# A hybrid decoder layer on one core: the last mean square on ScalarE, two weight tiles split earlier, and a pair of attention heads one tile later

## The chip, the core and the metric

The kernel runs on one core of a Trainium2 chip. The metric is the device time of one execution, in microseconds, as the median of several runs. The core's engines each work through their own list of instructions in order: TensorE (PE; PEld is its loading of the stationary operand), VectorE (DVE), ScalarE (ACT), GpSimd (POOL), and SyncE (SP), which here only starts DMAs. They wait for each other through semaphores.

## The reference

One decoder layer over 256 tokens of width 2048 in float32:

```
u   = RMSNorm_pre_mix(h);  P = u @ W_in      # z | x,B,C | dt | q | k | v
SSD half: conv + SiLU, chunked state space scan, gate, grouped RMSNorm
attention half, 16 heads of 128: softmax(q k / sqrt(128) + mask) v
h   = h + RMSNorm_post_mix(concat(SSD, attn) @ W_out)
h   = h + RMSNorm_post_mlp(relu(RMSNorm_pre_mlp(h) @ W_up)**2 @ W_down)

def rmsnorm(x, w):
    return x * rsqrt(mean(x * x, axis=-1) + 1e-6) * w
```

The three dilations of the attention are done as one softmax per head, with the logarithm of a key's count as its mask.

## The kernel before

**Products.** Every large product is made of three products of 32-bit operands that were rounded to a high part and a low part: high by high, high by low, low by high (`row_tile`, lines 323 to 325; `seven`, lines 406 to 408, uses a scheme with seven products for eight; `products`, lines 468 and 471, is the form with features on the partitions). So each weight tile of 256 rows by 512 columns goes through the same steps: `fetch` starts its DMA on SP's queue into one of four buffers `raw` (line 158), then `split` makes `hi` on ScalarE (line 144) and `lo` on VectorE (line 145). `parts` gives `hi` and `lo` out of five pairs of buffers, so ScalarE can run up to five tiles ahead of TensorE and then waits until TensorE has used the oldest.

**What sets the order.** Most of the program is put in order by a scheduler that follows priorities; weights have the highest. Two stretches are written out by hand, in an order that every engine keeps (`manual_schedule`): the start, and `mix_to_up`, the passage from the product with `w_out` to that with `w_up`.

**The heads.** `attention` is a generator that treats two heads at a time, in three stages: scores (lines 849, 850) and softmax (lines 857 to 863); the transposes of the softmax (line 871) and their copies; the product with v (lines 880, 881). `heads` puts two such pairs, called A and B below, into the list `waiting`. While a projection runs through its eight weight tiles, `gemm_features` calls `pump` after each tile, as often as the tuple `pumps` says (used in turn); each call takes one stage, of A and B in alternation. All of a pair's scores need both of the two small PSUM buffers (`psmall`), and so do its transposes.

**`mix_to_up`.** There are two tiles of 128 tokens, t = 0 and 1, and four blocks of 512 columns, n = 0 to 3. `out(t, i)` multiplies the last four tiles of `w_out`; `mix` adds that to what was there (line 1080); `mix_square` takes the sum of squares on ScalarE (line 1084); `weight` multiplies by the norm's weights (line 1087); `scale_of` turns the sums into the scale `rm` by a small VectorE operation (`mean`, line 1023) and a power on GpSimd (`rmix`, line 1024); `add` adds the scaled block to h (line 1091); `turn` transposes h on TensorE (line 1100); `take` splits it into the operand of the next product (lines 146, 147); `weigh(i)` fetches and splits tile i of `w_up`; `rows(t, i)` multiplies with it (lines 323 to 325 again). TensorE must have blocks of h to turn before it can begin with `rows`.

**`finish`.** After the very last product, `finish(t, acc)` adds the last block of columns (line 1309), takes its mean square together with the first three blocks' sum on VectorE (line 1311), takes the root on ScalarE and the reciprocal on VectorE (`inverse_root`, lines 1011 and 1012), multiplies the block by its weights in place (line 1313), scales everything, adds h (line 1326) and starts the output's DMAs. For t = 1 the first block of columns goes by ScalarE and TensorE (lines 1317 to 1323).

Of the kernel before, what the change touches and what calls it, by code (L numbers as in the profile page):

```python
# [13 lines left out]
AF = mybir.ActivationFunctionType  # L14
ALU = mybir.AluOpType
# [62 lines left out]
def hymba_layer(ctx: ExitStack, tc: tile.TileContext, x, norm_mix_pre, w_in, conv_w, conv_b, dt_bias, a_log,  # L78
# [909 lines left out]
    qk.append(keys_by_tokens(1, (0, 2, 1, 4, 3, 7, 5), (6,), *eight))  # L988
    vs = two_values(0, *eight[::-1])
    heads(0, *qk[0], vs[0])  # L990
    q2 = queries(COL_Q + 2 * NB, rbq, (1, 1, 0))
    drain()
    heads(1, *qk[1], vs[1])
    qk.append((q2, queries(COL_K + 2 * NB, rbc, (1, 1, 0))))
# [14 lines left out]
    def inverse_root(dst, m):  # L1009

        nc.scalar.activation(m, m, AF.Sqrt)
        nc.vector.reciprocal(dst, m)
# [42 lines left out]
    def mix_to_up(c0, ks, acc):  # L1055


        up = [bank() for _ in range(NT)]
        banks, turned = [], {}
        weighed = hp.tile([P, NT, NB], F32, name="e")  # L1060
        room_w = big.tile([P, SUMS, 2, S], F32R, name="ua").rearrange("p k b s -> p k (b s)")

        def tile_of(src, k, c0, at=None):
            raw = fetch(src, k * KB, c0)
            hi, lo = parts() if at is None else (room_w[:, at + KB * i:at + KB * (i + 1)] for i in range(2))
            split(hi, lo, raw)
            return hi, lo

        def out(t, i):
            row_tile(acc[1 + 2 * t], t, o[i], ks[i], part, False, i == len(ks) - 1)  # L1070

        def weigh(i):
            w[i] = tile_of(w_up, i % 8, i // 8 * NB)

        def rows(t, i):
            row_tile(up[t], t, w[i], i, act_u, i == 0, i == NK // KB - 1)

        def mix(t, n):
            m = mw_at(t, columns(n))
            nc.vector.tensor_tensor(m, acc[n - 2 + 2 * t], m, op=ALU.subtract if n % 2 else ALU.add)  # L1080

        def mix_square(t, n):
            junk = hp.tile([P, NB], F32, name="junk")
            nc.scalar.activation(junk, mw_at(t, columns(n)), AF.Square, accum_out=ssq[:, t, n:n + 1])

        def weight(t, n):
            nc.vector.tensor_mul(mw_at(t, columns(n)) if n == 2 else weighed[:, t], mw_at(t, columns(n)), wpost[n])

        def add(t, n):
            cs = columns(n)  # L1090
            nc.vector.scalar_tensor_tensor(of_h(t, cs), weighed[:, t] if n == 3 else mw_at(t, cs), rm[:, t:t + 1],
                                           of_h(t, cs), op0=ALU.mult, op1=ALU.add)

        def turn(t, n):
            if len(banks) < 3:
                banks.append([bank() if banks else psmall() for _ in range(2)])
            p = turned[t, n] = banks[len(turned) % 3]
            for f in range(4):
                k = 4 * n + f
                nc.tensor.transpose(p[f % 2][:, f // 2 * P:(f // 2 + 1) * P], of_h(t, slice(k * P, (k + 1) * P)), ident)  # L1100

        def take(t, i):
            for k in (2 * i, 2 * i + 1):
                f = k % 4
                split(*(u(k)[:, b, t * P:(t + 1) * P] for b in range(2)),
                      turned[t, k // 4][f % 2][:, f // 2 * P:(f // 2 + 1) * P], w_mlp[:, k:k + 1])

        def square(t, n):
            junk = hp.tile([P, NB], F32, name="junk")
            nc.scalar.activation(junk, of_h(t, columns(n)), AF.Square, accum_out=ssh[:, t, n:n + 1])  # L1110

        o, w = {}, {}
        with tc.high_priority(offset=AHEAD), tc.manual_schedule():
            o[0] = tile_of(w_out, ks[0], c0)
            with tc.issue_after(product[0].ins), tc.issue_after(product[1].ins):
                out(0, 0)
            o[1] = tile_of(w_out, ks[1], c0)
            out(0, 1)
            o[2] = tile_of(w_out, ks[2], c0, 0)
            o[3] = tile_of(w_out, ks[3], c0, 4)  # L1120
            mix(0, 2)
            mix_square(0, 2)
            out(0, 2)
            mix(1, 2)
            mix_square(1, 2)
            first3[0] = sums_but_last(ssq, 0)
            first3[1] = sums_but_last(ssq, 1)
            out(0, 3)
            mix(0, 3)
            weight(0, 2)  # L1130
            weigh(0)
            out(1, 0)
            mix_square(0, 3)
            out(1, 1)
            scale_of(rm, ssq, first3[0], 0)
            weigh(1)
            add(0, 0)
            out(1, 2)
            add(0, 1)
            turn(0, 0)  # L1140
            weigh(2)
            square(0, 0)
            out(1, 3)
            new_u()
            take(0, 0)
            square(0, 1)
            mix(1, 3)
            turn(0, 1)
            take(0, 1)
            take(0, 2)  # L1150
            rows(0, 0)
            mix_square(1, 3)
            rows(0, 1)
            scale_of(rm, ssq, first3[1], 1)
            add(0, 2)
            take(0, 3)
            add(1, 0)
            weigh(3)
            square(0, 2)
            weight(1, 3)  # L1160
            rows(0, 2)
            add(1, 1)
            square(1, 0)
            turn(1, 0)
            turn(0, 2)
            take(1, 0)
            rows(0, 3)
            take(0, 4)
            take(1, 1)
            turn(1, 1)  # L1170
            rows(1, 0)
            square(1, 1)
            rows(1, 1)
            weight(1, 2)
            take(1, 2)
            add(1, 2)
            weigh(4)
            turn(1, 2)
            add(1, 3)
            take(0, 5)  # L1180
            take(1, 3)
            rows(1, 2)
            rows(0, 4)
            turn(1, 3)
            square(1, 2)
            weight(0, 3)
            add(0, 3)
            take(1, 4)
            rows(1, 3)
            weigh(5)  # L1190
            take(1, 5)
            weigh(6)
            turn(0, 3)
            rows(1, 4)
            rows(0, 5)
            take(1, 6)
            square(0, 3)
            weigh(7)
            take(0, 6)
            rows(1, 5)  # L1200
            take(0, 7)
            square(1, 3)
            rows(1, 6)
            scale_of(rmlp, ssh, sums_but_last(ssh, 0), 0)
            rows(0, 6)
            weigh(8)
            take(1, 7)
            rows(0, 7)
            rows(1, 7)
            scale_of(rmlp, ssh, sums_but_last(ssh, 1), 1)  # L1210
        for t in range(NT):
            waiting.append(first_hidden(t, up[t]))
        pump(NT)
        return w[8]
# [87 lines left out]
    def finish(t, acc):  # L1302


        with tc.high_priority(offset=(1 + t) * AHEAD):
            cs = columns(3)
            m, some = (cp.tile([P, 1], F32, name="mean", bufs=2) for _ in range(2))
            nc.vector.tensor_scalar(some, first3[t], 1.0 / D, None, op0=ALU.mult)
            nc.vector.tensor_add(mw_at(t, cs), acc, mw_at(t, cs))
            junk = hp.tile([P, NB], F32, name="junk")  # L1310
            nc.vector.tensor_tensor_reduce(junk, mw_at(t, cs), mw_at(t, cs), 1.0 / D, some, ALU.mult, ALU.add, m)
            inverse_root(rff[:, t:t + 1], m)
            nc.vector.tensor_mul(mw_at(t, cs), mw_at(t, cs), wpost[3])
            if t:
                p = psmall()
                with tc.issue_after(product[t].ins):
                    nc.tensor.matmul(p, ident, of_h(t, columns(0)), start=True, stop=False)
                dg = cp.tile([P, P], F32, name="dg", bufs=2)
                nc.scalar.activation(dg, ident, AF.Copy, scale=rff[:, t:t + 1])
                nc.tensor.matmul(p, dg, mw_at(t, columns(0)), start=False, stop=True)  # L1320
                o = tmp()
                nc.scalar.activation(o, p, AF.Copy)
                nc.scalar.dma_start(ot[:, t, columns(0)], o)
            pieces = (slice(512, 768), slice(768, 1024), slice(1024, 1536), slice(1536, 2048))
            for n, cs in enumerate(pieces if t else (columns(0), *pieces)):
                nc.vector.scalar_tensor_tensor(of_h(t, cs), mw_at(t, cs), rff[:, t:t + 1], of_h(t, cs),
                                               op0=ALU.mult, op1=ALU.add)
                (nc.sync if t else (nc.sync, nc.scalar)[n % 2]).dma_start(ot[:, t, cs], of_h(t, cs))
# [133 lines left out]
```

## Time and profile before

| what | value |
|---|---|
| median of 3 runs | 1464.41 us (1463.12 to 1464.65) |
| the profiled execution: its own time | 1462.01 us |
| its span, first to last instruction | 1460.1 us |
| granted TensorE clock, mean | 0.999 |
| TensorE busy | 1451.3 us, 99% of the span |
| VectorE busy | 1254.7 us, 86% |
| ScalarE busy | 888.7 us, 61% |
| GpSimd busy | 143.1 us, 10% |

The stretches that the change touches lie, on the profile's axis from the span's start, at 446 to 474 us (the first two pairs of heads), at 757 to 800 us (`mix_to_up`) and from 1446 us to the end (`finish`). A row of the timeline reads: start, duration, engine, line, operation, written tile <- read tiles, shapes, and in brackets how long the engine had been idle and what ended that. A matmul's duration is its whole way through the array, 0.39 us for 512 columns, while one starts every 0.23 us; so TensorE loses more in a gap than the bracket shows.

### The profile page before, as it was taken

How to read it: one execution, taken by the hardware profiler on the slowest of the kernel's cores; microseconds unless marked ns; L12 is line 12 of the kernel's file. 1: busy time of each engine (PE TensorE's matmuls, PEld its weight loads, DVE VectorE, ACT ScalarE, POOL GpSimd, SP SyncE). 2: the span in 40 equal slices, each digit the busy share in tenths (PEclk: the TensorE clock that was granted, in tenths of full speed). 3: DMA queues.
4: the chain of work that ended last, by engine and by line, in shares of the span. 5: the costliest groups of instructions: out<-in, count | busy, mean ns of one | idle time of the engine just before them, and what ended most of it. 6: DMA issues, size and time to landing. Idle time of an engine off the chain costs nothing.

```text
span 1460.1 us, 20264 instructions
## 1 busy us (share of the span) xinstructions
PE 1451.3 (99%) x7129; PEld 1223.8 (84%) x7129; DVE 1254.7 (86%) x1864; ACT 888.7 (61%) x1214; POOL 143.1 (10%) x208
## 2 busy tenths in 40 slices
PE   9999999999999999999999999999999999999998
PEld 8888888888888888888887888888888888888886
DVE  6798797898887686689979999988889999999987
ACT  7475675465566555555557677655455776766553
POOL 0003100212010000000100011000111111001000
PEclk9999999999999999999999999999999999999999
DMA  8766666666886586688867798778888888797763
GB/s 273 209 204 180 180 184 192 175 180 184 226 241 206 134 245 199 192 265 253 253 190 241 202 315 240 217 214 230 246 236 271 263 244 250 204 308 238 251 212 116
DMA packets 168039, 323.53 MB, mean 222 GB/s; under 512 B 15185, under 2 KB 18113, under 8 KB 167937
## 3 DMA queue, kind: packets, MB, share of 16 engines
q1 hardware_dynamic: 144448, 272.37, 59.0%
q0 software_dynamic: 15616, 36.19, 12.3%
q10 hardware_dynamic: 7872, 13.68, 2.8%
q8 instruction: 56, 0.92, 0.2%
q14 instruction: 47, 0.38, 0.1%
HBM read 317.96 MB, written 40.41 MB: 245 GB/s over the span
## 4 chain that ended last, share of the span: by engine, by line
PE 99%; DVE 1%; ACT 0%; issue 0%; POOL 0%
PE acc L468 15%; PE acc L323 12%; PE acc L325 12%; PE acc L324 12%; PE acc L471 8%; PE acc L408 6%; PE acc L407 6%; PE acc L406 6%; PE ps L325 3%; PE ps L323 3%; PE ps L324 3%; PE ps L406 2%; PE ps L408 2%; PE ps L407 2%; PE ps L802 1%; PE acc L1375 1%
## 5 line engine op out<-in xcount | busy, mean ns | idle before, releaser
L144 ACT ACTIVATE hi<-raw 128x1024 fp32r<-128x1024 f32 (+1 forms) x408 | 427.1, 1051 | 293.0 <-PE acc L325 93.9
L145 DVE TENSOR_TENSOR lo<-raw,hi 128x1024 fp32r<-128x1024 f32 (+1 forms) x408 | 496.2, 1220 | 103.8 <-ACT hi L144 99.2
L468 PE MATMUL acc<-ua,hi 128*128 128x512 f32 x600 | 163.4, 401 | 0.0
L468 PEld LDWEIGHTS acc<-ua,hi 128*128 128x128 f32 x600 | 105.7, 189 | 16.7
L144 ACT ACTIVATE hi<-e 128x1024 fp32r<-128x1024 f32 x61 | 64.9, 1063 | 73.8 <-DVE e L247 67.4
L323 PE MATMUL acc<-hi,ua 128*128 128x512 f32 x248 | 98.5, 397 | 0.0
L471 PEld LDWEIGHTS acc<-ua,lo 128*128 128x128 f32 x600 | 88.2, 189 | 10.2
L325 PE MATMUL acc<-hi,ua 128*128 128x512 f32 x248 | 96.8, 390 | 0.0
L324 PE MATMUL acc<-lo,ua 128*128 128x512 f32 x248 | 96.7, 390 | 0.0
L471 PE MATMUL acc<-ua,lo 128*128 128x256 f32 x600 | 90.8, 281 | 0.0
L323 PE MATMUL acc<-hi,sh 128*128 128x512 f32 x224 | 88.4, 395 | 0.0
L325 PE MATMUL acc<-hi,sl 128*128 128x512 f32 x224 | 87.3, 390 | 0.0
L324 PE MATMUL acc<-lo,sh 128*128 128x512 f32 x224 | 87.2, 389 | 0.0
L145 DVE TENSOR_TENSOR lo<-e,hi 128x1024 fp32r<-128x1024 f32 x61 | 74.2, 1217 | 0.0
L468 PE MATMUL acc<-uc,hi 128*128 128x512 f32 x240 | 68.4, 397 | 0.0
L406 PE MATMUL acc<-hi,ah 128*128 128x512 f32 x166 | 64.7, 389 | 0.0
L407 PE MATMUL acc<-lo,ah 128*128 128x512 f32 x166 | 64.6, 389 | 0.0
L408 PE MATMUL acc<-hi,al 128*128 128x512 f32 x166 | 64.6, 389 | 0.0
L325 PE MATMUL acc<-hi,al 128*128 128x512 f32 x148 | 57.6, 389 | 0.0
L323 PE MATMUL acc<-hi,ah 128*128 128x512 f32 x148 | 57.6, 389 | 0.0
L324 PE MATMUL acc<-lo,ah 128*128 128x512 f32 x148 | 57.6, 389 | 0.0
L325 PEld LDWEIGHTS acc<-hi,ua 128*128 128x128 f32 x248 | 46.6, 188 | 10.0
(533 smaller groups left out, 3436.4 us busy)
## 6 DMA issues: line engine op xcount, KB each, us to landing
raw<-in_w_in_dram SPq DMA_DIRECT2D x181, 512.0 KB, 4.0
raw<-in_w_down_dram SPq DMA_DIRECT2D x73, 512.0 KB, 5.0
raw<-in_w_up_dram SPq DMA_DIRECT2D x65, 512.0 KB, 4.8
raw<-in_w_out_dram SPq DMA_DIRECT2D x39, 512.0 KB, 4.9
pair<-in_w_up_dram POOLq DMA_DIRECT2D x56, 256.0 KB, 5.3
raw<-pair SPq DMA_DIRECT2D x46, 256.0 KB, 4.5
pair<-in_w_down_dram POOLq DMA_DIRECT2D x46, 256.0 KB, 5.9
ha<-in_w_up_dram SPq DMA_DIRECT2D x20, 512.0 KB, 5.1
```

Of the source, the lines that this page charges most:

```text
L144: return (nc.scalar.activation(hi, src, AF.Copy), nc.vector.tensor_tensor(lo, src, hi.bitcast(F32), op=ALU.subtract))
L145: nc.vector.tensor_tensor(lo, src, hi.bitcast(F32), op=ALU.subtract))
L323: nc.tensor.matmul(dst, a_h[:, r, ts], hi[:, j], start=begin and j == 0, stop=False)
L324: nc.tensor.matmul(dst, a_h[:, r, ts], lo[:, j], start=False, stop=False)
L325: product[t] = nc.tensor.matmul(dst, a_l[:, r, ts], hi[:, j], start=False, stop=end and j == KB - 1)
L406: nc.tensor.matmul(dst, a_h, hi[:, j], start=own and first, stop=False)
L407: nc.tensor.matmul(dst, a_h, lo[:, j], start=False, stop=False)
L408: nc.tensor.matmul(dst, a_l, hi[:, j], start=False, stop=own and last)
L468: nc.tensor.matmul(acc[f], hi[:, j, f * P:(f + 1) * P], u(k0 + j), start=k0 + j == 0, stop=False, skip_group_check=True)
L471: nc.tensor.matmul(acc[f][:, 0], lo[:, j, f * P:(f + 1) * P], u(k0 + j)[:, 0], start=False, stop=k0 + j == NK - 1, skip_group_check=True)
L802: nc.tensor.matmul(p[:, c, r], bc[:, r, c * P:(c + 1) * P], xdt[:, c, r], start=True, stop=True)
L1375: nc.tensor.transpose(p[:, f * P:(f + 1) * P], r[:, f * P:(f + 1) * P], ident)
```

## The change

Three edits, in three places.

1. While the third block of queries is projected, the stages of the pairs A and B are taken after tiles 0, 2, 3, 5, 6 and 7 instead of 0, 1, 3, 4, 6 and 7.
2. In `mix_to_up`, tiles 0 and 1 of `w_up` are fetched and split ahead of the last block `out(0, 3)`, not behind `weight(0, 2)` and `scale_of`.
3. In `finish`, the sum of squares is taken by ScalarE (Square with an accumulated sum) and not by VectorE; the division by D and the other blocks' sum go into the root's scale and bias; the reciprocal now stands behind the multiplication by the weights.

```
-    q2 = queries(COL_Q + 2 * NB, rbq, (1, 1, 0))
+    q2 = queries(COL_Q + 2 * NB, rbq, (1,0,1,1,0,1,1,1))
...
             first3[1] = sums_but_last(ssq, 1)
+            weigh(0)
+            weigh(1)
             out(0, 3)
             mix(0, 3)
             weight(0, 2)
-            weigh(0)
             out(1, 0)
             mix_square(0, 3)
             out(1, 1)
             scale_of(rm, ssq, first3[0], 0)
-            weigh(1)
             add(0, 0)
...
-            nc.vector.tensor_tensor_reduce(junk, mw_at(t, cs), mw_at(t, cs), 1.0 / D, some, ALU.mult, ALU.add, m)
-            inverse_root(rff[:, t:t + 1], m)
+            nc.scalar.activation(junk, mw_at(t, cs), AF.Square, accum_out=m)
+            nc.scalar.activation(m, m, AF.Sqrt, scale=1.0 / D, bias=some)
             nc.vector.tensor_mul(mw_at(t, cs), mw_at(t, cs), wpost[3])
+            nc.vector.reciprocal(rff[:, t:t + 1], m)
```

SP's and GpSimd's lists stay as they were; so the DMAs of `w_up` start in the same order. One line is added, so lines behind 1311 count one more afterwards.

VectorE's list in `mix_to_up`, before (-) and now (+). `lo<-raw,hi` are the low parts of w_up's tiles 0, 1 and 2; line 1080 is `mix(0, 3)`, line 1087 `weight(0, 2)`, line 1023 the mean for t = 0, line 1091 `add(0, 0)` and `add(0, 1)`:

```order
 L1017 TENSOR_REDUCE some<-ssq 128x1
 L1018 TENSOR_SCALAR some<-some 128x1
+L145 TENSOR_TENSOR lo<-raw,hi 128x1024 x2
 L1080 TENSOR_TENSOR mw_6121<-acc,mw_6121 128x512
 L1087 TENSOR_TENSOR mw_6120<-mw_6120,wpost 128x512
-L145 TENSOR_TENSOR lo<-raw,hi 128x1024
 L1023 TENSOR_SCALAR mean<-ssq,some 128x1
-L145 TENSOR_TENSOR lo<-raw,hi 128x1024
 L1091 SCALAR_TENSOR_TENSOR ha<-mw_6119,rmix,ha 128x512 x2
 L145 TENSOR_TENSOR lo<-raw,hi 128x1024
```

Both low parts have moved from behind the wait for TensorE's last block (line 1080) to ahead of it, and none stands between that block and the mean, or between the mean and the first `add`, any more.

VectorE's list at the end of `finish` for t = 1, before, with what each row waits for. `mean` is the variable m, `mw_10232` the last block:

```order
L1309 TENSOR_TENSOR mw_10232<-acc,mw_10232 128x512 [waits PE_49]
L1311 ISA junk,mean<-mw_10232,mean 128x512 [waits DVE_49]
L1311 ISA mean 128x1
L1313 TENSOR_TENSOR mw_10232<-mw_10232,wpost 128x512 [waits DVE_49]
L1012 RECIPROCAL rff<-mean 128x1 [waits Activation_49]
```

The same place now, on VectorE:

```order
L1309 TENSOR_TENSOR mw_10232<-acc,mw_10232 128x512 [waits PE_49]
L1313 TENSOR_TENSOR mw_10232<-mw_10232,wpost 128x512 [waits Activation_49]
L1314 RECIPROCAL rff<-mean 128x1 [waits Activation_49]
L1327 SCALAR_TENSOR_TENSOR ha<-mw_6119,rff,ha 128x256 [waits DVE_49]
L1327 SCALAR_TENSOR_TENSOR ha<-mw_6119,rff,ha 128x256
```

And on ScalarE now:

```order
L1311 ACTIVATE junk,mean<-mw_10232 128x512 [waits DVE_49,Activation_49]
L1312 ACTIVATE mean<-mean 128x1 [waits Activation_49]
L1320 ACTIVATE dg<-ident,rff 128x128 [waits DVE_49]
L1323 ACTIVATE r<-ps 128x512 [waits PE_49]
L1324 DMA out_dram<-r 128x512 [waits DMAHW7_49,Activation_49]
```

The product with the weights writes over the block that ScalarE reads, so it waits for ScalarE where it waited for VectorE's own sum of squares before.

TensorE's list at the first heads: B's scores (lines 849, 850) move behind one more weight tile (lines 468, 471):

```order
 L468 MATMUL acc<-ua,hi 128x512 x8
 L471 MATMUL acc<-ua,lo 128x256 x8
+L468 MATMUL acc<-ua,hi 128x512 x8
+L471 MATMUL acc<-ua,lo 128x256 x8
 L849 MATMUL ps<-cT 128x128
 L850 MATMUL ps<-cT 128x256
```

A's transposes (line 871, the first of them in the next piece) stay behind the fourth tile, and now come one tile after B's scores and not two; B's transposes move one tile back.

More of the change, by code (lines that the diff above doesn't have):

```diff
@@ L990, in hymba_layer @@
     heads(0, *qk[0], vs[0])
-    q2 = queries(COL_Q + 2 * NB, rbq, (1, 1, 0))
+    q2 = queries(COL_Q + 2 * NB, rbq, (1,0,1,1,0,1,1,1))
     drain()
@@ L1127, in mix_to_up @@
             first3[1] = sums_but_last(ssq, 1)
+            weigh(0)
+            weigh(1)
             out(0, 3)
@@ L1130, in mix_to_up @@
             weight(0, 2)
-            weigh(0)
             out(1, 0)
@@ L1135, in mix_to_up @@
             scale_of(rm, ssq, first3[0], 0)
-            weigh(1)
             add(0, 0)
@@ L1310, in finish @@
             junk = hp.tile([P, NB], F32, name="junk")
-            nc.vector.tensor_tensor_reduce(junk, mw_at(t, cs), mw_at(t, cs), 1.0 / D, some, ALU.mult, ALU.add, m)
-            inverse_root(rff[:, t:t + 1], m)
+            nc.scalar.activation(junk, mw_at(t, cs), AF.Square, accum_out=m)
+            nc.scalar.activation(m, m, AF.Sqrt, scale=1.0 / D, bias=some)
             nc.vector.tensor_mul(mw_at(t, cs), mw_at(t, cs), wpost[3])
+            nc.vector.reciprocal(rff[:, t:t + 1], m)
             if t:
```

## The prediction

> **What bounds the kernel now.** I read the page first, then TensorE's waits, then the timeline of the three stretches that the change touches. The page says that TensorE is nearly always at work, and that the chain that ended last is TensorE's own work:
>
> ```profile
> PE 1451.3 (99%) x7129; PEld 1223.8 (84%) x7129; DVE 1254.7 (86%) x1864; ACT 888.7 (61%) x1214; POOL 143.1 (10%) x208
> ...
> PE 99%; DVE 1%; ACT 0%; issue 0%; POOL 0%
> ```
>
> The change takes no matmul away, so it can only win or lose time in which TensorE waits. The list of TensorE's waits is short (who waited <- for whom: us in total, times, longest):
>
> ```profile
> PE ps L1320 <- ACT dg L1319: 2.0, 1, 2.0
> PE ps L519 <- DVE half L508: 1.1, 1, 1.1
> PE ps L1100 <- DVE ha L1091: 1.0, 1, 1.0
> PE acc L1100 <- DVE ha L1091: 0.2, 1, 0.2
> ```
>
> The first lies in `finish`, the second is the start, and the last two lie in `mix_to_up`, where TensorE waits to transpose h. The heads (lines 849 to 881) are not in the list: TensorE waits for nothing there. So edit 2 can win little more than one microsecond, edit 1 nothing, and edit 3 acts on the tail, where all engines wait in a row.
>
> **Edit 2, `mix_to_up`.** This is TensorE at the wait:
>
> ```profile
> 766.38 0.39 PE L324 MATMUL acc<-ua,ah 128*128 128x512 f32 x1
> 766.61 0.39 PE L325 MATMUL acc<-ua,al 128*128 128x512 f32 x1
> 767.95 0.66 PE L1100 MATMUL ps<-ident,ha 128*128 128x128 f32 x4 [0.95 <-DVE ha L1091]
> ```
>
> Matmuls start 0.23 us apart (766.38 to 766.61), so the next one could have started at 766.84; it started at 767.95. The stall is worth 1.11 us. It ends with VectorE's `add(0, 0)`, and this is VectorE ahead of it:
>
> ```profile
> 762.95 0.69 DVE L1080 TENSOR_TENSOR mw<-acc,mw 128x512 f32<-128x512 f32 x1 [3.56 <-PE acc L325]
> 763.56 0.68 DVE L1087 TENSOR_TENSOR mw<-mw,wpost 128x512 f32<-128x512 f32 x1
> 764.16 1.22 DVE L145 TENSOR_TENSOR lo<-raw,hi 128x1024 fp32r<-128x1024 f32 x1
> 765.29 0.21 DVE L1023 TENSOR_SCALAR mean<-ssq,some 128x1 f32<-128x1 f32 x1
> 765.45 1.23 DVE L145 TENSOR_TENSOR lo<-raw,hi 128x1024 fp32r<-128x1024 f32 x1
> 767.14 1.42 DVE L1091 SCALAR_TENSOR_TENSOR ha<-mw,rmix,ha 128x512 f32<-128x512 f32 x2 [0.47 <-POOL rmix L1024]
> ```
>
> VectorE sits idle for 3.56 us, then the block arrives, and only then does it make the low part of tile 0 (1.22 us), with the mean behind it. The mean could have run when ScalarE's sum was read:
>
> ```profile
> 758.93 1.04 ACT L144 ACTIVATE hi<-raw 128x1024 fp32r<-128x1024 f32 x1
> 763.74 0.63 ACT L1084 ACTIVATE junk<-mw 128x512 f32<-128x512 f32 x1 [3.77 <-DVE mw L1080]
> 764.27 0.19 ACT L1084 ACTIVATION_READ_ACCUMULATOR junk<-mw 128x1 f32 x1
> 764.37 1.99 ACT L144 ACTIVATE hi<-raw 128x1024 fp32r<-128x1024 f32 x2
> ```
>
> That is 764.27 + 0.19 = 764.46, so with 0.03 for the signal the mean starts at 764.49 and not at 765.29: 0.80 us earlier. Then comes GpSimd's power. Its rows, for t = 0 here and for the later norm:
>
> ```profile
> 765.59 1.51 POOL L1024 TENSOR_TENSOR rmix<-mean,half 128x1 f32<-128x1 f32 x1 [29.98 <-DVE mean L1023]
> 792.17 0.54 POOL L1024 TENSOR_TENSOR rmlp<-mean,half 128x1 f32<-128x1 f32 x1 [17.94 <-DVE mean L1023]
> ```
>
> The same operation on one column took 1.51 us while VectorE split tile 1 beside it (765.45 to 766.68), and 0.54 us at 792.17. After the change nothing stands on VectorE between the mean and `add(0, 0)`, which waits for this very result, so VectorE is idle and I take 0.54, the row with the nearer conditions; 1.51 stays as the other end. Then: mean 764.49 to 764.70, power from 764.79 (0.09 after, as before) to 765.33, `add(0, 0)` from 765.37 to 766.11, TensorE released at 766.18 (0.07 after the add's end, as before). TensorE is busy until 766.84. The whole stall of 1.11 us goes, with 0.66 us in hand. With 1.51 for the power, TensorE would start at 767.15 and the gain would be 0.80 us. The Trainium skill, in "SBUF — State Buffer", section "SBUF: two separate sides", says that a VectorE operation with two inputs in SBUF and a GpSimd operation that reads SBUF exclude each other for a whole instruction. The trace agrees: the slow power ended 0.42 us behind the split beside which it ran; by that page the sum is the 1.11, without it the 0.80.
>
> What of the moved work must fit into the idle 3.56 us: ScalarE makes the high part of tile 0 at 758.93 as before, and that of tile 1 right behind it, from 759.88 to 760.92 (two such take 1.99, so 0.95 apart); VectorE's low parts then run from 760.00 to 761.22 and from 761.14 to 762.36. `mix(0, 3)` is due at 762.95, so 0.59 us is left. Tile 1 must have landed by 759.88. Its DMA is the second of `w_up`; the second row is the view by windows (busy PE, PEld, DVE, ACT, POOL with counts, then clock, share of the DMA engines, GB/s):
>
> ```profile
> 752.63 0.37 SPq L158 DMA_DIRECT2D raw<-in_w_up_dram  x1
> ...
> 760.00:765.00 5.00, 5.00 (x23) 4.13 (x22) 2.05 (x3) 1.26 (x3) 0.00 (x0) 1.00 0.02 7
> ```
>
> The DMA engines are busy for 0.02 of the time from 760 to 765, so all that was started before had landed, tile 1 included. SP's order does not change; the buffers of tiles 0 and 1 come free earlier, so tiles 4 and 5 are fetched about four microseconds earlier, into a stretch in which the DMA engines are idle.
>
> What is late next: `take(0, 0)` overwrites a buffer that `out(1, 3)` reads, so it starts when TensorE has finished that block, and everything up to `turn(1, 0)`, with the wait of 0.2 us that is the last row of the list of waits, hangs on TensorE. It moves along and keeps its length. So edit 2 gives -1.1 us, with bounds of 0 (tile 1 late) and -1.5 (the second stall goes too: 0.2 in the list, and 0.16 more by starts, as the first is 1.11 against 0.95).
>
> **Edit 3, `finish`.** This is the critical end for t = 1, VectorE and ScalarE:
>
> ```profile
> 1451.62 0.69 DVE L1309 TENSOR_TENSOR mw<-acc,mw 128x512 f32<-128x512 f32 x1 [0.20 <-PE acc L325]
> 1452.34 0.75 DVE L1311 CUSTOM_DVE_ANT_0 junk<-mw,mean 128x512 f32<-128x512 f32 x1
> ...
> 1453.14 0.69 DVE L1313 TENSOR_TENSOR mw<-mw,wpost 128x512 f32<-128x512 f32 x1
> 1453.20 0.20 ACT L1011 ACTIVATE mean<-mean 128x1 f32<-128x1 f32 x1 [5.31 <-DVE mean L1311]
> 1453.75 0.15 DVE L1012 RECIPROCAL rff<-mean 128x1 f32<-128x1 f32 x1
> ```
>
> The root already runs beside the product with the weights; the reciprocal waits in VectorE's queue until that product is through. From the start of the add to the start of the product pass 1.52 us. In the new order the product still waits, now for ScalarE, since it overwrites what ScalarE reads. The same pattern (add, Square with a sum on ScalarE, product with the weights in place) stands 10 us earlier:
>
> ```profile
> 1440.25 1.28 DVE L1415 TENSOR_TENSOR mw<-acc,mw 128x512 f32<-128x512 f32 x2
> 1440.97 0.63 ACT L1417 ACTIVATE junk<-mw 128x512 f32<-128x512 f32 x1 [1.89 <-DVE mw L1415]
> 1441.51 0.19 ACT L1417 ACTIVATION_READ_ACCUMULATOR junk<-mw 128x1 f32 x1
> 1441.73 0.69 DVE L1418 TENSOR_TENSOR mw<-mw,wpost 128x512 f32<-128x512 f32 x1 [0.19 <-ACT junk L1417]
> ```
>
> From add to product there: 1441.73 - 1440.25 = 1.48 us. Where ScalarE waits for two semaphores, as it will here, the Square began 0.10 us behind the add's end (763.74 against 762.95 + 0.69) and not 0.04, which makes 1.54. Against 1.52 that is -0.04 to +0.02. The root follows the read of the sum by about 0.1 us and takes 0.20, so it is done 0.4 us before the product. For t = 0 the same few hundredths are covered by TensorE, since VectorE waits 0.20 us for it ahead of t = 1 (first row above). I take 0. Bounds: -0.61, if the product did not wait for ScalarE (the reciprocal starts 1453.75 - 1453.14 behind the product's start), and +0.2, one more small ScalarE step like the root's 0.20.
>
> **Edit 1, the heads.** TensorE does the same work in another order; a gain is excluded, because it waits for nothing there. Can it lose? These rows give the pace (PE: B's scores, the first and the second tile behind them, A's transposes; then ScalarE's high part, which waits until TensorE has let go of a buffer; then VectorE):
>
> ```profile
> 451.00 0.39 PE L849 MATMUL ps<-cT 128*128 128x128 f32 x2
> ...
> 452.12 0.58 PE L468 MATMUL acc<-ua,hi 128*128 128x512 f32 x1
> ...
> 455.11 2.00 PE L468 MATMUL acc<-ua,hi 128*128 128x512 f32 x8
> ...
> 457.91 0.82 PE L871 MATMUL ps<-ident,sm 128*128 128x128 f32 x6
> ...
> 454.41 1.06 ACT L144 ACTIVATE hi<-raw 128x1024 fp32r<-128x1024 f32 x1 [1.14 <-issue]
> ...
> 449.75 0.28 DVE L857 CUSTOM_DVE_ANT_0 sm<-ps,cst 128x128 f32<-128x128 f32 x1
> ...
> 450.86 0.08 DVE L857 DVE_READ_ACCUMULATOR2_ANT mx<- 128x1 f32 x1
> ...
> 457.50 0.55 DVE L863 TENSOR_SCALAR sm<-sm,den 128x128 f32<-128x128 f32 x2
> ```
>
> A tile takes 2.80 us (455.11 to 457.91). B's scores, which take 1.12 (451.00 to 452.12), move one tile back, to 453.80, and end at 454.92; A's transposes stay at 457.91, and they need the two small buffers that B's scores fill. In that time VectorE must make a low part, finish A's softmax and read B's scores. The high part ahead of that low part waits for the tile that began at 452.12 and now begins at 451.00; so it comes 1.12 earlier, at 453.29, is done at 454.35, and the low part (1.22) at 455.6. Behind it stand the rest of A's softmax (one scaling, half of the 0.55 for two; then a reciprocal, 0.15 as in `finish`, and two scalings, 0.55) and B's four reads (449.75 to 450.94 for A's, so 1.19): 455.6 + 2.2 = 457.8. The transposes need the second buffer from the fourth of six on, at about 458.2. So it fits, with 0.3 us in hand: 0 us, with +1.2, one split, as the bad end.
>
> **Sum.** -1.1 + 0 + 0 = -1.1 us. The profiled execution took 1462.01 us for its span of 1460.1; with the change I expect 1460.9 for such a one. The three runs lie higher, at 1464.41 in the median, so the prediction is 1464.41 - 1.1 = 1463.3. It is 0.08% less. I count as no change what lies within 0.2% (2.9 us), about what a measurement of this kernel can tell from no change.
>
> **The rivals.**
>
> *The heads come late (slower).* If VectorE is one split and a little more (over 1.4 us) later than worked out when it reads B's scores, it eats the 0.3 in hand and then the 1.1 that edit 2 wins. Two splits late (2.4 us) would cost 2.1 and end at 1463.3 + 2.1 = 1465.4, slower than before. For it: ScalarE now has a high part that waits for TensorE ahead of A's last exponentials, so that a delay would pass on. Against it: the wait of 1.14 us in ScalarE's row ends with TensorE, which is 1.1 us earlier there. 0.10.
>
> *Edit 2 does nothing.* If tile 1 came to ScalarE over 0.6 us late, its low part would push `mix(0, 3)`, as it pushes the mean now, and the time would stay at 1464.4. For it: three loads run at once there. Against it: the idle DMA engines from 760 on. 0.08.
>
> *Edit 3 does what its name says.* If the product ran beside the sum of squares, the tail would be 0.6 us shorter: 1462.7. For it: the change's words. Against it: the wait in the order. 0.05.
>
> **How the numbers follow.** The forecast has 0.72; 0.05 is left for what I don't see. All these cases lie within 2.9 us of 1464.41. The range takes the lowest run less the largest gain of edit 2, 1463.12 - 1.5 = 1461.6, and the highest run with the heads one split late less 0.8 from edit 2, 1464.65 + 1.2 - 0.8 = 1465.05, so 1465.1. To be faster by over 0.2%, two thirds of all waits in TensorE's list (4.3 us) would have to go: 0.05. To be slower by over 0.2%, the heads would have to be four microseconds late, or something unseen: 0.05. That leaves 0.90.
>
> **What would show it.** Right: TensorE's wait L1100 <- DVE ha of 1.0 us is gone, GpSimd's first `rmix` takes about 0.54 us, VectorE's idle time ahead of line 1080 shrinks to about 0.6 us, TensorE's wait for `dg` stays at 2.0 us, and no wait on lines 849 to 881 appears. Wrong: a wait on line 871 or 849, ScalarE idle for a DMA at tile 1, or a wait for `dg` well below 2.0.

## The result and the profile after

The changed kernel takes 1462.13 us in the median of 22 runs (1460.59 to 1463.91); the kernel before, in 22 runs beside it, takes 1464.43 us (1462.21 to 1468.18). The ratio is 0.9982, with an interval of 0.9976 to 0.9989: 2.6 us less (1.6 to 3.5). The forecast was 1.1 us less. The spread has changed too: 15 of the 22 runs of before are longer than the longest run of after.

The profiled execution of after took 1461.61 us for its span of 1459.7. Its busy times and its chain, from the page:

```profile
PE 1451.7 (99%) x7129; PEld 1224.1 (84%) x7129; DVE 1254.1 (86%) x1860; ACT 890.3 (61%) x1218; POOL 142.1 (10%) x208
...
PE 99%; DMA 0%; DVE 0%; ACT 0%; SPq 0%; issue 0%; ACTq 0%
```

TensorE's waits in it (who waited <- for whom: us in total, times, longest):

```profile
PE ps L1321 <- ACT dg L1320: 2.0, 1, 2.0
PE ps L519 <- DVE half L508: 1.1, 1, 1.1
PE acc L1100 <- DVE ha L1091: 0.2, 1, 0.2
PE ps L549 <- DMA xs<-in_x_dram: 0.2, 1, 0.2
```

Against the list of before only the 1.0 us at line 1100 is gone; the wait for `dg` is still 2.0. By these two profiled executions the change is worth 0.40 us (1462.01 to 1461.61), by the medians 2.3 us. So one of the two is not typical, and the question for the runs is where the rest comes from. (The 1.11 us that edit 2 wins does not show whole in the 0.40, as the execution of after came to the first heads' scores 0.65 us later than that of before: 447.54 against 446.89.)

**`mix_to_up` after.** The timeline of VectorE, GpSimd and TensorE, one after the other:

```profile
761.00 2.36 DVE L145 TENSOR_TENSOR lo<-raw,hi 128x1024 fp32r<-128x1024 f32 x2 [0.61 <-ACT hi L144]
763.95 0.69 DVE L1080 TENSOR_TENSOR mw<-acc,mw 128x512 f32<-128x512 f32 x1 [0.58 <-PE acc L325]
764.56 0.68 DVE L1087 TENSOR_TENSOR mw<-mw,wpost 128x512 f32<-128x512 f32 x1
765.49 0.21 DVE L1023 TENSOR_SCALAR mean<-ssq,some 128x1 f32<-128x1 f32 x1 [0.25 <-ACT junk L1084]
766.39 1.42 DVE L1091 SCALAR_TENSOR_TENSOR ha<-mw,rmix,ha 128x512 f32<-128x512 f32 x2 [0.69 <-POOL rmix L1024]
...
765.79 0.57 POOL L1024 TENSOR_TENSOR rmix<-mean,half 128x1 f32<-128x1 f32 x1 [27.98 <-DVE mean L1023]
...
767.60 0.39 PE L325 MATMUL acc<-ua,al 128*128 128x512 f32 x1
767.84 0.60 PE L1100 MATMUL ps<-ident,ha 128*128 128x128 f32 x4
```

Both low parts run while VectorE would have waited for the block, and the mean comes 0.93 us behind `weight` (765.49 - 764.56) where it came 1.73 behind it. GpSimd's power takes 0.57 us where it took 1.51. TensorE starts to transpose 0.24 us behind the matmul ahead of it: the stall of 1.11 us has gone as a whole.

**`finish` after**, VectorE and ScalarE for t = 1:

```profile
1451.22 0.69 DVE L1309 TENSOR_TENSOR mw<-acc,mw 128x512 f32<-128x512 f32 x1 [0.17 <-PE acc L325]
1452.01 0.63 ACT L1311 ACTIVATE junk<-mw 128x512 f32<-128x512 f32 x1 [4.39 <-DVE mw L1309]
...
1452.76 0.69 DVE L1313 TENSOR_TENSOR mw<-mw,wpost 128x512 f32<-128x512 f32 x1 [0.85 <-ACT junk L1311]
1452.76 0.29 ACT L1312 ACTIVATE mean<-mean 128x1 f32<-128x1 f32 x1
1453.37 0.16 DVE L1314 RECIPROCAL rff<-mean 128x1 f32<-128x1 f32 x1
```

VectorE sits idle for 0.85 us and begins the product when ScalarE is through with the block: 1.54 us behind the start of the add, where it was 1.52. The sum of squares has changed engines and has not moved beside the product.

**The heads after.** TensorE (scores of A, the two tiles, scores of B, A's transposes), then VectorE:

```profile
447.54 0.38 PE L849 MATMUL ps<-cT 128*128 128x128 f32 x2
...
454.44 0.39 PE L849 MATMUL ps<-cT 128*128 128x128 f32 x2
...
458.62 1.10 PE L871 MATMUL ps<-ident,sm 128*128 128x128 f32 x6
...
451.52 1.23 DVE L145 TENSOR_TENSOR lo<-raw,hi 128x1024 fp32r<-128x1024 f32 x1 [0.95 <-ACT hi L144]
452.67 0.28 DVE L857 CUSTOM_DVE_ANT_0 sm<-ps,cst 128x128 f32<-128x128 f32 x1
```

VectorE's first read of A's scores (line 857) starts 5.13 us behind the scores (452.67 - 447.54); in the profile of before it started 2.86 us behind them (449.75, with A's scores at 446.89). TensorE doesn't wait for it, since B's scores now stand 6.90 us behind A's. Had this execution run in the old order, with B's scores 4.11 us behind A's (446.89 to 451.00), TensorE would have had to wait. That gave the theory below.

### The profile page after: what moved, and what is told of

It reads as the page before. It is cut to its first block, busy times and chain, and to the rows that moved or that the text cites. A ratio compares the mean times of both kernels' runs of the same rounds, so it can differ in the third digit from the quotient of the medians.

```text
span 1459.7 us, 20266 instructions
## 1 busy us (share of the span) xinstructions
PE 1451.7 (99%) x7129; PEld 1224.1 (84%) x7129; DVE 1254.1 (86%) x1860; ACT 890.3 (61%) x1218; POOL 142.1 (10%) x208
## 4 chain that ended last, share of the span: by engine, by line
PE 99%; DMA 0%; DVE 0%; ACT 0%; SPq 0%; issue 0%; ACTq 0%
PE acc L468 15%; PE acc L323 12%; PE acc L325 12%; PE acc L324 12%; PE acc L471 8%; PE acc L406 6%; PE acc L408 6%; PE acc L407 6%; PE ps L323 3%; PE ps L325 3%; PE ps L324 3%; PE ps L406 2%; PE ps L408 2%; PE ps L407 2%; PE ps L802 1%; PE acc L1376 1%
```

## The experiments

My theory: in most executions of before TensorE waits at B's scores. VectorE's reads of A's scores stand in its list behind a low part whose weights arrive late, and the profiled execution was one in which they came early. Edit 1 gives B's scores one tile more and so removes a wait of 1 to 3 us that the profile of before did not show. The rival: the profile of before is typical, edit 1 is worth nothing, and the additional gain comes from edit 2 or 3, or lies in the noise.

**Each edit alone**, on the kernel before, and a second profile of the kernel before itself.

```
heads_only:   q2 = queries(COL_Q + 2 * NB, rbq, (1,0,1,1,0,1,1,1))
split_only:   weigh(0); weigh(1) ahead of out(0, 3)
finish_only:  Square with sum on ScalarE, product, reciprocal
before_again: no edit
```

> Edit 1 alone: the stages of the pairs A and B one tile further apart. Theory 1 (most executions of the kernel before stall at B's scores, because VectorE reads A's scores behind a low part whose weights came late, and the profiled execution was a lucky one): 1.0 to 2.0 us faster in the median, and no wait on line 849. Theory 2 (edit 1 wins nothing, as predicted): within 0.5 us of before, perhaps 0.25 slower by a wait at A's transposes.

> Edit 2 alone: tiles 0 and 1 of w_up split ahead of the last block of w_out. Theory 1: 1.1 us faster, the wait L1100 <- DVE ha of 1.0 us gone, the first rmix in 0.5 to 0.6 us. Theory 2, by which edit 2 has the whole gain: 2.0 to 2.6 us faster in the median.

> Edit 3 alone: the last mean square on ScalarE. Theory 1 and 2: no difference (within 0.3 us), the wait for dg stays at 2.0 us. Rival (ScalarE's sum shortens or lengthens the tail): 0.3 us or more either way, with the wait for dg changed by as much.

> The kernel before once more, for a second profile of it. Theory 1: TensorE waits 1 to 2 us at line 849 or near it, between 446 and 475 us, where the first profile shows none. Theory 2: the waits of the first profile again (2.0, 1.1, 1.0 and 0.2 us) and nothing on the heads' lines.

Against before (1464.53 us, 29 runs beside them):

| kernel | median, us | lowest to highest | ratio | interval |
|---|---|---|---|---|
| heads_only | 1463.02 | 1461.88 to 1464.19 | 0.9989 | 0.9981 to 0.9998 |
| split_only | 1463.47 | 1462.19 to 1467.55 | 0.9991 | 0.9981 to 1.0001 |
| finish_only | 1463.80 | 1462.07 to 1467.16 | 1.0000 | 0.9990 to 1.0009 |
| before_again | 1464.41 | one run | | |

The wait is there in all three of these profiles that keep the old order of the heads. From TensorE's waits in split_only, finish_only and before_again, a fence each:

```profile
PE ps L849 <- DVE mx L857: 2.6, 1, 2.6
```

```profile
PE ps L849 <- DVE mx L857: 2.4, 1, 2.4
```

```profile
PE ps L849 <- DVE mx L857: 1.5, 1, 1.5
```

It is missing in heads_only and after, though VectorE reads A's scores late in heads_only as well, 4.6 us behind them (the scores start at 447.09):

```profile
450.55 1.23 DVE L145 TENSOR_TENSOR lo<-raw,hi 128x1024 fp32r<-128x1024 f32 x1 [0.88 <-ACT hi L144]
451.69 0.28 DVE L857 CUSTOM_DVE_ANT_0 sm<-ps,cst 128x128 f32<-128x128 f32 x1
```

The timeline of before_again shows the chain, first ScalarE, then VectorE, then TensorE:

```profile
444.87 1.06 ACT L144 ACTIVATE hi<-raw 128x1024 fp32r<-128x1024 f32 x1 [3.30 <-DMA raw<-in_w_in_dram]
...
451.55 1.23 DVE L145 TENSOR_TENSOR lo<-raw,hi 128x1024 fp32r<-128x1024 f32 x1 [0.95 <-ACT hi L144]
452.69 0.28 DVE L857 CUSTOM_DVE_ANT_0 sm<-ps,cst 128x128 f32<-128x128 f32 x1
...
447.61 0.38 PE L849 MATMUL ps<-cT 128*128 128x128 f32 x2
...
453.38 0.49 PE L849 MATMUL ps<-cT 128*128 128x128 f32 x2 [1.51 <-DVE mx L857]
```

ScalarE sits idle for 3.30 us until weights land and is late with the tiles behind them; the low part ahead of the reads waits for ScalarE; the reads start 5.08 us behind A's scores; B's scores start 0.69 us behind the first of the reads (453.38 - 452.69). So the old order, with 4.11 us between the two scores, bore reads up to 4.11 - 0.69 = 3.4 us behind A's scores, and the new one, with 6.90, bears 6.2. The profile of before had 2.86 and didn't stall; before_again 5.08, finish_only 5.96 and split_only 6.19 did, and all three would fit into the new order, the last with nothing to spare. What they exceed the 3.4 by, 1.7, 2.5 and 2.8 us, is what their lists show as waits (1.5, 2.4 and 2.6) with about 0.15 added, as 1.11 us by starts stood against 0.95 in the bracket at line 1100. Edit 2 alone takes the wait of 1.0 us at line 1100 away (split_only's list has only the second one there, of 0.2) and is worth 1.3 us by its ratio, though its interval still holds no gain at all; edit 3 alone is worth nothing, and its wait for `dg` is 2.0.

**What a long wait costs beside itself.** The profiled execution of split_only took 1465.47 us and that of finish_only 1464.73, though split_only's wait is only 0.2 us longer and it no longer loses the 1.1 us at line 1100. The traces show why. Behind the wait of 2.62 us in split_only the clock that TensorE was granted fell to 0.50, and the eight matmuls of line 468 behind B's scores took 3.77 us; behind the wait of 2.38 us in finish_only the clock stayed at 1.00, and they took 2.20. First split_only (TensorE, then the view by windows, with clock, share of the DMA engines and GB/s at the end), then finish_only:

```profile
455.37 3.77 PE L468 MATMUL acc<-ua,hi 128*128 128x512 f32 x8
...
456.00:457.00 1.00, 1.00 (x3) 0.72 (x3) 1.00 (x5) 0.95 (x5) 0.00 (x0) 0.50 0.65 250
...
455.14 2.20 PE L468 MATMUL acc<-ua,hi 128*128 128x512 f32 x8
```

From 455 to 459 us the clock of split_only was 0.57 in the mean, so about 1.7 us of those 4 were lost on top of the wait. The runs fit: with the old order of the heads (split_only, finish_only and the three sets of runs of before) 8 of 87 have a mean clock of 0.997, and all eight take 1465.47 us or more; of the 65 runs of the kernels without the wait (heads_only and after, and three that come below) none has. That the clock fell behind the same wait in the other seven is not shown, since only split_only's has a trace. A lower clock by itself is not what makes the old order slow: without the wait, the runs at 0.998 take 1462.6 us in the mean and those at 0.999 take 1462.4.

**The queue, without moving the scores.** If VectorE's list is the cause, it must do to let the reads go first, with the old stages; the other edits can then be added, with the product in `finish` freed from ScalarE's read.

```
reads_first (on before):
+  with tc.high_priority(offset=2 * AHEAD):
       nc.vector.tensor_tensor_reduce(sm[:, cs], s[:, cs], mk, ...)
product_beside (on after):
-  nc.vector.tensor_mul(mw_at(t, cs), mw_at(t, cs), wpost[3])
+  last = tmp()
+  nc.vector.tensor_mul(last, mw_at(t, cs), wpost[3])
   (and the scaling of the last block reads last)
all_and_reads: before + edits 2 and 3 + product_beside + reads_first
```

> The kernel before with its old stages, but VectorE's reads of the scores have a higher priority than the low parts, so that A's reads stand ahead of the low part that came late. Theory (TensorE's wait at line 849 is VectorE's queue: the reads behind a late low part): that wait is gone and the median is 1.0 to 2.0 us faster than before, as with edit 1 alone. Rival (late weights stop TensorE by themselves, wherever the reads stand): the wait moves to lines 468 or 471, and the time stays within 0.5 us of before.

> The changed kernel, but the last product with the weights writes to a buffer of its own, so that it need not wait for ScalarE's reading. Theory (the wait is due to writing over what ScalarE reads): the product starts 0.1 us after the add, the reciprocal follows ScalarE's root, and TensorE's wait for dg falls from 2.0 to 1.7 us. Rival (the sum of squares is late, not the product): the wait stays at 2.0 us.

> Edits 2 and 3, the product with the weights in its own buffer, and the reads first with the old stages. Theory: 1.1 us from edit 2, about 1.5 from the reads, 0.3 from the product: 2.5 to 3.2 us faster than before, about 1461.6, at or a little below the changed kernel.

Against before (1464.61 us, 20 runs): reads_first takes 1462.63 us (1462.00 to 1464.97), ratio 0.9989 (0.9980 to 0.9998), the same as heads_only, and its list has no wait at line 849. In its profile ScalarE sat idle even longer for weights, and yet VectorE's first read of A's scores (line 858, as one line is added) starts only 2.93 us behind them (the scores start at 447.18), since a low part that stood ahead of it now stands behind:

```profile
444.46 1.06 ACT L144 ACTIVATE hi<-raw 128x1024 fp32r<-128x1024 f32 x1 [3.73 <-DMA raw<-in_w_in_dram]
...
450.11 0.28 DVE L858 CUSTOM_DVE_ANT_0 sm<-ps,cst 128x128 f32<-128x128 f32 x1
```

So the order on VectorE is the cause, and moving the scores is one of two cures. product_beside was profiled once, at 1462.16 us. Its waits on TensorE:

```profile
PE ps L1322 <- ACT dg L1321: 1.7, 1, 1.7
...
PE ps L871 <- DVE mx L857: 0.3, 1, 0.3
```

With the product in another buffer it does run beside the sum of squares, and the wait for `dg` shrinks by 0.3 us. That is what the words of edit 3 promise and the edit itself doesn't reach. It is half of the 0.6 that the rival had put on it. all_and_reads takes 1461.30 us (1460.49 to 1462.64), ratio 0.9977 (0.9968 to 0.9986). By its median it is the best of all, 0.8 us below after; the intervals of the two ratios overlap.

**Why the weights come late.** In the profile of before, GpSimd starts the second of the two DMAs that gather a pair of w_out's tiles 14.2 us ahead of A's scores, and in before_again 11.0 us ahead (the timeline of GpSimd, each of its own kernel):

```profile
432.70 0.81 POOL L272 DMA_DIRECT2D pair<-in_w_out_dram  x1 [5.10 <-DMA pair<-in_w_out_dram]
```

```profile
436.65 0.82 POOL L272 DMA_DIRECT2D pair<-in_w_out_dram  x1 [6.37 <-DMA pair<-in_w_out_dram]
```

The loads of w_in that are in flight with it should then be the late ones. The kernel before without this one gather tells (both of its DMAs are left out, so the product that uses this pair reads old data):

```
one_gather_less (on before, in next_pair):
+  if len(paired) == 8:
+      paired.append((src, ca, k, d))
+      return
   (ahead of the two DMAs)
```

> The kernel before, without the two GpSimd DMAs that gather pair no. 8, the first pair of w_out's weights; the product that uses it reads old data instead, so the output is not the reference's. All else stands in the old order. My theory (the weights of the tile ahead of A's scores land late because that gather is in flight with them, and VectorE then reads A's scores behind a low part that waits for those weights): the loads started 10 to 5 us ahead of A's scores land within 5 us instead of 5.3 to 7.2, TensorE's wait L849 <- DVE mx is gone or below 0.5 us, and the median is 1 to 1.5 us below that of before. The rival (the loads are late for another reason, or the low part stands ahead of the reads whatever the loads do): they still take over 5.3 us, or TensorE's wait at L849 stays at 1 to 2.6 us, and the time is that of before within 0.5 us.

It takes 1462.76 us (1461.97 to 1464.04) against 1464.05 for before (15 runs), ratio 0.9991 (0.9982 to 1.0000), and has no wait at A's and B's scores (line 852 there). The loads started from 434 to 445 us, from the view of the DMAs (count, KB each, median us from issue to landing), for before_again and for one_gather_less:

```profile
raw<-in_w_in_dram SPq DMA_DIRECT2D x4, 512.0 KB, 6.6
pair<-in_w_out_dram POOLq DMA_DIRECT2D x1, 256.0 KB, 7.4
```

```profile
raw<-in_w_in_dram SPq DMA_DIRECT2D x5, 512.0 KB, 4.7
```

VectorE's first read of A's scores there (line 860, as three lines are added; the scores start at 447.15):

```profile
450.03 0.28 DVE L860 CUSTOM_DVE_ANT_0 sm<-ps,cst 128x128 f32<-128x128 f32 x1
```

That is 2.88 us behind the scores, as in the profile of before (2.86). The gather in flight makes the loads late, and the loads make the wait. The profile of before is the odd one: in the ten other profiles of kernels that have this gather, GpSimd starts its second DMA 9.7 to 11.9 us ahead of A's scores, and the loads of that stretch take 5.2 to 7.0 us in the median; in before it started 14.2 us ahead, and they took 4.5. What makes GpSimd early in one execution and late in another was not tried. In before_again it was already 2.5 us later when it started the first of the two DMAs (429.46 against 426.95), and 3.1 us later at a gather some ten microseconds ahead (417.82 against 414.75), so most of the delay is older than the rows above; on top of it GpSimd waits longer for the first of the two to land (6.37 us against 5.10).

**The slow power.** Two kernels were to have work of VectorE beside GpSimd's power again: split_tile0, which is the kernel before with half of edit 2, and low1_beside, which is the kernel after with one low part put back.

```
split_tile0 (on before):  weigh(0) ahead of out(0, 3), weigh(1) behind scale_of
low1_beside (on after):   high part of tile 1 ahead of out(0, 3),
                          its low part on VectorE behind scale_of
```

> Half of edit 2: tile 0 of w_up goes ahead of the last block, tile 1 stays behind scale_of, so that its low part runs on VectorE beside GpSimd's power. Theory (the power waits for a VectorE operation with two inputs in SBUF): rmix again takes 1.4 to 1.6 us, the mean comes 0.8 us earlier than before, and TensorE's wait at line 1100 shrinks from 1.0 to 0.1 to 0.3 us. Rival (the power is slow for another reason that edit 2 as a whole removed): rmix takes 0.5 to 0.6 us and the wait is gone.

> The kernel after, but the low part of w_up's tile 1 is put on VectorE right behind the mean, where it runs beside GpSimd's power as it did before the change; its high part is still made ahead of out(0, 3), so that it has not to be waited for. My theory (the power is slow because VectorE reads two inputs in SBUF beside it): the first rmix takes 1.3 to 1.6 us and ends about 0.4 us behind the low part; TensorE's wait at L1100 comes back with 0.1 to 0.4 us. The rival (the power was slow for another reason, being the first after a long pause): rmix takes 0.5 to 0.6 us though the low part runs beside it; the low part then sets when add(0, 0) starts.

split_tile0 (1463.38 us, one run) told nothing about the power: ScalarE made the high part so late that the low part began at 767.52, behind the power's end (766.87 + 0.57 = 767.44). So the power had nothing beside it, and TensorE's wait at line 1100 was 0.4 us and not the 0.1 to 0.3 that were expected. But split_tile0 keeps the old order of the heads, and VectorE reads A's scores 4.64 us behind them (447.67 to 452.31), so it is one more profile with the wait:

```profile
PE ps L849 <- DVE mx L857: 1.1, 1, 1.1
```

low1_beside (1462.66 us, one run) has the two side by side. VectorE, GpSimd and TensorE in its timeline:

```profile
765.38 0.21 DVE L1023 TENSOR_SCALAR mean<-ssq,some 128x1 f32<-128x1 f32 x1 [0.25 <-ACT junk L1084]
765.51 1.22 DVE L1139 TENSOR_TENSOR lo<-raw,hi 128x1024 fp32r<-128x1024 f32 x1
767.20 1.42 DVE L1091 SCALAR_TENSOR_TENSOR ha<-mw,rmix,ha 128x512 f32<-128x512 f32 x2 [0.47 <-POOL rmix L1024]
...
765.68 1.48 POOL L1024 TENSOR_TENSOR rmix<-mean,half 128x1 f32<-128x1 f32 x1 [28.64 <-DVE mean L1023]
...
767.50 0.39 PE L325 MATMUL acc<-ua,al 128*128 128x512 f32 x1
768.00 0.66 PE L1100 MATMUL ps<-ident,ha 128*128 128x128 f32 x4
```

The power takes 1.48 us again and ends 0.43 us behind the low part, as it ended 0.42 behind it in before. With nothing beside it, it took 0.57. So the time of the power is set by what VectorE does meanwhile. This agrees with the rule that the prediction took from the Trainium skill ("SBUF — State Buffer", section "SBUF: two separate sides"): 1.48 us is the rest of the low part, 1.05, plus 0.43. The profile of before has a further case, at t = 1: the power there started at 773.23 beside an `add` that ended at 773.81, took 1.00 us, and ended 0.42 behind it. TensorE pays little for the slow power: its transpose starts 0.50 us behind the matmul ahead of it, so 0.27 are lost where the prediction's other end had 0.31 (1.11 - 0.80). The wait at line 1100 that was expected in the list is too short to be there.

## Why the prediction was right, and where not

**Right.** 1462.13 lies in the range of 1461.6 to 1465.1, near its lower end, and the change is within 0.2% of before, the case that had 0.90. Both are in part luck. By the runs of each edit alone, more than half of the 2.6 us comes from edit 1, for which the prediction had excluded a gain; the range holds it only because its lower end starts from the lowest of the three runs.

**Edit 2: as worked out.** The predicted stall of 1.11 us is gone; the power took 0.57 against 0.54; VectorE's idle time ahead of line 1080 is 0.58 against 0.59; the second stall stayed at 0.2. Alone the edit gave 1.3 us by the runs, with an interval of -0.1 to 2.8. The bound with a power of 1.51 did not come true, and low1_beside shows that it would have, had the low part stayed beside it (0.27 us lost against 0.31).

**Edit 3: as worked out.** The product waits for ScalarE, 1.54 us behind the add (1.48 to 1.54 was the forecast), the wait for `dg` stays at 2.0, and alone the edit gave 0 +- 1.4 us. The root takes 0.29 us with its scale and bias and not the 0.20 of before, which the product hides.

**Edit 1: the failed step.** "TensorE does the same work in another order; a gain is excluded, because it waits for nothing there." It waits there, 1.1 to 2.6 us, in four of the five profiled executions that have the old order on TensorE and VectorE and all gathers; the one that the prediction read took 1462.01 us, less than the lowest of the 22 runs beside after (1462.21) and 2.4 less than the median that the prediction itself started from. That gap stood in the prediction ("The three runs lie higher") and was carried along as a constant, when most of it was a wait that the profile did not hold: before_again, at 1464.41, has 1.7 us of it between A's and B's scores (453.38 - 447.61 against 4.11) and 0.7 ahead of A's. Alone the edit gave 1.6 us (0.3 to 2.8); with the 1.1 of edit 2 that makes 2.7, against 2.6 measured. The spread says the same: the longest runs of the kernels that still have the wait (before in each set of runs, split_only, finish_only) are 1466.58 us and more, those of the kernels without it (heads_only, reads_first, one_gather_less, all_and_reads, after) 1464.97 and less.

**The 0.3 us in hand at A's transposes** were used up. VectorE was 2.3 us later at A's scores than in the profile of before, and six transposes take 1.10 us in after where they took 0.82; the list of product_beside names what they wait for, the reads of B's scores. This loss of about 0.3 us is covered by the wait that went; the first rival, the heads late and the time above 1464.4, needed far more. That ScalarE's high part there waits for TensorE was the prediction's reading of the program; the row that it shows names no releaser (`<-issue`).

## What to carry to other kernels

Before a wait is called absent, set the profiled execution's own time beside the runs: if it is lower by more than the step in dispute, the profile may be without a wait that other executions have, and a second profile costs little. Look then for a list in which something that TensorE will soon need stands behind work that waits for a DMA: either take it out of that queue or put more of TensorE's work ahead of its use. And work that changes engine runs beside its neighbour only if the neighbour doesn't overwrite what it reads.

## What was not expected of the hardware

- A wait of 1.5 us on TensorE comes in one execution of a program and not in another, at nearly the same clock (0.998 and 0.999). It hangs on when a DMA of 256 KB, the second half of a gather, was started, some 11 or 14 us earlier: loads of 512 KB land in 6.6 us in the median with it in flight, and in 4.7 with the gather left out.
- After a wait of 2.62 us TensorE's granted clock fell to 0.50, and to 0.57 in the mean of 4 us, which cost about 1.7 us more (split_only); after waits of 2.38 us (finish_only) and 1.51 us (before_again) it stayed at 1.00.
- A power on one column took 0.57 us on GpSimd with VectorE idle and 1.48 beside a VectorE operation of 1.22 us, though neither needs the other's data.
